# Score products with full-height rests in an fp32 diffusion-transformer kernel

## The chip, the cores and the metric

The kernel runs on one core of one Trainium2 chip. The metric is device time in microseconds (us): the median of several executions. One further execution was recorded by the hardware profiler; its span runs from its first to its last instruction.

## What is computed

Two layers of a hybrid backbone over 256 latent and 256 context tokens of width 1024, all fp32. Each layer modulates its input (adaLN), projects it once, and splits the result into three head groups of 64-wide heads: A (6 query heads on 2 key heads, a window of 128 tokens and a per-head sink), B (4 heads, a neighbourhood with a relative bias), C (6 query heads on 2 key heads, global, normalised queries and keys). Latent queries also see all context keys; context queries see context keys alone. An output projection, a norm, and a mixture of 16 experts follow. The part that the change touches is the first line of each attention:

```python
s = jnp.einsum('bqhgd,bkhd->bhgqk', q_i, k_all, preferred_element_type=jnp.float32) * scale
p = jax.nn.softmax(s, -1).astype(v.dtype)
return jnp.einsum('bhgqk,bkhd->bqhgd', p, v_all).reshape(bsz, Q_BLOCK, n_heads * HEAD_DIM)
```

In the second (last) layer no context queries are needed.

## The kernel before, in words

Large products run in the type fp32r. To keep fp32's digits, an operand is split into a head (its value rounded to fp32r) and a rest (what rounding left over), and products of the parts are added in one PSUM bank. The three products of `mm3` (L221 to L223) are head by head, head by rest and rest by head. The weights are split by `split_w`: ScalarE casts 1024 columns to the head `wh` (L211), VectorE subtracts it to give the rest `wl` (L212). Both lie in the pool `wsp`, which holds three such pairs, and each pair serves two of the eight contraction steps of a projection, for four token tiles of 128.

Projection comes in the order V, A, C, B. For each token tile, `finish` rotates and normalises queries and keys, splits them into `hl`, transposes `hl` in blocks of 128 columns on PE (L725, up to four blocks in one bank `qtp`) and evicts them into `qkA`, `qkB` or `qkC`. A query head takes one block, in which the 64 rows of its head and the 64 rows of its rest stand one above the other, the head on top for even heads and below for odd ones. A key head takes one block with its head twice, so a single product over 128 rows gives (query head + query rest) by key head. The key rests stand once, two key heads to a block. The second score product takes only the 64 rows with the query's head and the key's rest (L523); `kv % 2` says which half.

For one head and one block of 128 queries, `products` writes one bank `s`. For latent queries (`nb == 1`) it holds 512 keys: L516 is the first product, for group A L520 adds the window's mask as a bf16 product, and L523 is the second. Context queries (`nb == 2`, layer 0 alone: banks A2, A3, C2, C3, B2) have two query blocks of 256 keys each in one bank. `scores` takes the maximum on VectorE (L535) and the exponential on ScalarE (L546). `values` transposes the probabilities in four pieces (L559, bank `ptp`), copies them (L490 on ScalarE, one in six L492 on VectorE) and multiplies by the values in 16 products with 64 columns each (L568). `blocks` keeps two or three heads pending between the two. The adaLN products (L366, 32 columns) are put between. With `PAIRS="B"`, group B of layer 1 issues the products of two heads before their scores.

The output projection reads its weights in eight pieces `w_half`: the first three are split into `wsp` as attention ends, the others into buffers of their own (L911), each ordered behind the last attention transposes (`otp`, L865, cast at L868). For the experts, buffers that are free by then become 15 slots of 1 MB for weights: three of them are the pairs of `wsp`, one is `ringc`.

The order on each engine is not written by hand: the framework orders the program by a simulated timeline, under the dependencies and priorities given, and any change of the code orders it anew.

Of the kernel before, what the change touches and what calls it, by code (L numbers as in the profile page):

```python
# [17 lines left out]
F32 = mybir.dt.float32  # L18
F32R = mybir.dt.float32r
# [4 lines left out]
ALU = mybir.AluOpType  # L24
# [4 lines left out]
P = 128  # L29
# [18 lines left out]
RING_B = 4  # L48
WS_UNITS = 3
VECS_AHEAD = 2  # L50
# [8 lines left out]
P_BUFS = 3  # L59
KN = [dict(ADA=("10101010", "00100100", "01010101", "01", "110"), AHEAD=(2, 3, 2), EVAC="VSSSSS", PAIRS=""), dict(ADA=("01010101", "01010101", "11110000", "10", "0"), AHEAD=(2, 3, 2), EVAC="VSSSSS", PAIRS="B")]  # L60
REST_G = ((1, 2, 3), (0, 1))
# [48 lines left out]
def layers(ctx: ExitStack, tc: tile.TileContext, x_in, x_ctx, c_in, w_in, w_out, w_ada, rows_in, lnv, sink, gains, rpbp,  # L110
# [12 lines left out]
    ringu = ctx.enter_context(tc.tile_pool(name="ringu", bufs=RING_U))  # L123
    wsp = ctx.enter_context(tc.tile_pool(name="wsp", bufs=3))
    sm = ctx.enter_context(tc.tile_pool(name="sm", bufs=6))
# [329 lines left out]
    def pre_moe(l, sb, sr):  # L455
# [5 lines left out]
        with ExitStack() as st, ExitStack() as su:  # L461
            with ExitStack() as sa:
# [39 lines left out]

                def products(ps, bk, hs):

                    grp, b, nb = bk.grp, bk.b, bk.nb
                    qk, nq = qkt[grp], heads[grp]
                    tiles = [ps.tile([P, 512], F32, tag="s", name="s") for _ in hs]
                    k = slice(0, 512) if nb == 1 else slice(256, 512)  # L510
                    for c in range(nb):
                        q = slice((b + c) * P, (b + c + 1) * P)
                        each = [(h, h if grp == "B" else h % 2, s if nb == 1 else s[:, c * 256:(c + 1) * 256])
                                for h, s in zip(hs, tiles)]
                        for h, kv, so in each:
                            T.matmul(so, qk[:, h, q], qk[:, nq + kv, k], start=True, stop=False)  # L516
                        if nb == 1 and grp == "A":
                            o = 128 * (1 - b)
                            for s in tiles:
                                T.matmul(s[:, o:o + 128], identb, maskb[:, b], start=False, stop=False)  # L520
                        for h, kv, so in each:
                            r = slice(64 * (kv % 2), 64 * (kv % 2) + 64)
                            T.matmul(so, qk[r, h, q], qk[r, 8 + kv // 2, k], start=False, stop=True)  # L523
                    return tiles

# [65 lines left out]
                def blocks(keys, depth):  # L591

                    for key in keys:
                        if key in banks:
                            bk = Bank(key)
                            n = 2 if bk.grp in KN[l]["PAIRS"] else 1
                            for h0 in range(bk.h0, bk.h1, n):
                                hs = range(h0, h0 + n)
                                for h, s in zip(hs, products(now["ps"], bk, hs)):
                                    pend.append((bk, h, scores(bk, h, s)))  # L600
                                    drain(now["ps"], now["po"], depth)
                                    yield

# [6 lines left out]
                with ExitStack() as sp:  # L610
# [68 lines left out]
                    def finish(grp, t, src, lo, rs=None):  # L679
# [5 lines left out]
                        if grp not in qkt:  # L685
                            qkt[grp] = ap_.tile([P, 10, N_TOK], F32R, tag="qkC" if grp == "C" else "qkAB",
                                                name=f"qk{grp}")
                        if grp == "A" and t < 2:
                            src = rope(src, t, 0, 8, cosx[:, t], sinx[:, t])
                        elif grp == "C":  # L690
                            for h0, h1, i in ((0, 6, 0), (6, 8, 2)):
# [7 lines left out]
                                else:  # L699
# [5 lines left out]
                                    [P, n, HD]), op=ALU.mult)  # L705
                        hl = wq.tile([P, 1280], F32R, tag="hl", name="hl")
                        if lo == 0:
# [8 lines left out]
                        S.copy(hh, sv.unsqueeze(2).to_broadcast([P, nk, 2, HD]))  # L716
                        V.tensor_tensor(out=hl[:, kd:kd + nk * HD].rearrange("p (h d) -> p h d", d=HD), in0=sv,
                                        in1=hh[:, :, 0].bitcast(F32), op=ALU.subtract)
                        a = 0 if lo == 0 else nq
                        n = 8 + nk // 2  # L720
                        while a < n:
# [174 lines left out]
            def w_half(kt):  # L896
                if kt % 2 == 0:
                    whl.append(unit(w_out[l, kt // 2]))
                w = whl[kt // 2][:, kt % 2 * 1024:kt % 2 * 1024 + 1024]
                if kt < 3:  # L900

                    hl = split_w(w)
                    for split, last_of in zip((keep["cast"], keep["split"]), heads_done[kt - 3]):
                        order(split, last_of, mybir.DependencyClass.NoSync)
                    return hl
# [350 lines left out]
    def moe(l, ringb, gen, rt, u2d, aff, nt, sb, ahead):  # L1256
        cap = CAP[l]
        with ExitStack() as st:
            mp = st.enter_context(tc.tile_pool(name="moe", bufs=1, side="right"))
            ringc = st.enter_context(tc.tile_pool(name="ringc", bufs=1))  # L1260
            m1 = st.enter_context(tc.tile_pool(name="moe1", bufs=2))
# [15 lines left out]
            for e in range(NE - 2):  # L1277
# [4 lines left out]
            slots = [(ring, "w")] * RING_A + [(ringu, "wu")] * (RING_U - 1) + [(ringb[0], "wb")] + [  # L1282
                (ringb[1], "wb")] * (RING_B - 1) + [None] * WS_UNITS + [(ringc, "wb"), (ringu, "wu")]
            n_slots = len(slots)
# [347 lines left out]
```

## Time and profile before

| | us |
|---|---|
| median of 3 runs | 1159.81 |
| lowest and highest | 1156.51, 1160.08 |
| the profiled execution | 1151.46 |
| its span | 1149.6 |
| PE busy | 1032.0 (90%) |
| VectorE (DVE) busy | 518.2 (45%) |
| ScalarE (ACT) busy | 330.1 (29%) |
| GpSimd (POOL) busy | 257.0 (22%) |

The mean granted clock of TensorE is 0.962. Each row of a timeline is an instruction (or several alike): its start, its length, engine, line, operation, output and inputs by the program's names, the shape of the weights x the moving operand, and in brackets the idle time before it and what ended it. `64*128 64x512` is a product with weights of 64 rows and 128 columns and 512 moving columns. PEld is the load of weights, which can run under a product. In the waits, `A <- B: 1.6, 1, 1.6` says that A waited for B 1.6 us in total, in one wait, the longest of 1.6 us.

### The profile page before, as it was taken

To read this page: it belongs to the slowest core of one execution; us is meant where nothing else is said; L and a number is where in the kernel's file an instruction comes from. 1 tells how busy PE (TensorE), PEld (TensorE's weight loads), DVE (VectorE), ACT (ScalarE), POOL (GpSimd) and SP (SyncE) were. 2 spreads that over 40 slices of the span, in tenths; PEclk is the share of its full clock that TensorE was granted. 3 is DMA by queue.
4 is the path that set the end of the run, shared out by engine and by line. 5 is a ranking of instruction groups with operands and counts; after the bars stand their busy time and mean duration, and the time that the engine had idled before them with its cause. 6 is when DMAs were issued, how large, how long until landed. Compare 5 with 4: busy or idle time off the path is not lost. (4 is left out here: it accounts for less than half of the span.)

```text
span 1149.6 us, 21044 instructions
## 1 busy us (share of the span) xinstructions
PE 1032.0 (90%) x8651; PEld 598.5 (52%) x8652; DVE 518.2 (45%) x1221; ACT 330.1 (29%) x688; POOL 257.0 (22%) x238
## 2 busy tenths in 40 slices
PE   5899999999968999999997799999995999878775
PEld 3677666667854444444443478666673333322222
DVE  2525655557782443443433644655865122211115
ACT  1334457456121110110111543446632001000002
POOL 3000000100004244244233300001001455434142
PEclk9999999999988999999999799999996999989997
DMA  9855442864698999999996345574398999999992
GB/s 315 314 191 157 141 146 76 295 229 182 233 418 272 371 369 361 375 347 337 344 370 247 131 147 193 188 257 144 118 381 336 328 395 394 397 393 392 407 390 85
DMA packets 67345, 320.93 MB, mean 279 GB/s; under 512 B 14894, under 2 KB 19086, under 8 KB 38312
## 3 DMA queue, kind: packets, MB, share of 16 engines
q1 hardware_dynamic: 50304, 289.21, 66.2%
q0 software_dynamic: 11136, 23.30, 7.7%
q10 hardware_dynamic: 5800, 6.97, 1.8%
q8 instruction: 71, 1.16, 0.4%
q14 instruction: 34, 0.28, 0.1%
HBM read 310.40 MB, written 18.15 MB: 286 GB/s over the span
## 5 line engine op out<-in xcount | busy, mean ns | idle before, releaser
L1184 PE MATMUL ha<-w,xT 128*32 128x512 f32 (+1 forms) x1512 | 251.1, 604 | 22.1 <-DMA w<-in_w_dram 21.7
L1184 PEld LDWEIGHTS ha<-w,xT 128*32 128x32 f32 (+1 forms) x1512 | 74.4, 121 | 165.3 <-issue 117.0
L1211 ACT ACTIVATE hs<-ha 64x512 f32<-64x512 f32 x32 | 18.9, 592 | 403.4 <-PE ha L1184 403.4
L1184 PE MATMUL ya<-w,gT 128*32 128x512 f32 (+1 forms) x768 | 128.3, 597 | 2.7 <-DVE y L1231 1.6
L221 PE MATMUL pj<-wh,u 128*128 128x512 f32 (+2 forms) x256 | 95.1, 384 | 5.1 <-ACT wh L211 3.8
L222 PE MATMUL pj<-wl,u 128*128 128x512 f32 (+2 forms) x256 | 96.2, 377 | 0.6 <-DVE wl L212 0.5
L223 PE MATMUL pj<-wh,u 128*128 128x512 f32 (+2 forms) x256 | 93.2, 376 | 0.0
L1156 POOL MEMSET xg<- 96x1024 f32 (+1 forms) x32 | 30.2, 947 | 216.2 <-PE tp L1169 133.5
L1253 POOL DMA_INDIRECT ysum<-y,ii x30 | 44.2, 1474 | 148.1 <-DVE y L1234 98.9
L1231 DVE TENSOR_TENSOR y<-ya,gt 64x512 f32<-64x512 f32 x60 | 41.3, 688 | 78.8 <-PE ya L1184 71.2
L535 DVE TENSOR_REDUCE mx<-s 128x1 f32<-128x512 f32 (+1 forms) x80 | 54.7, 690 | 42.4 <-PE s L523 41.6
L212 DVE TENSOR_TENSOR wl<-w,wh 128x1024 fp32r<-128x1024 f32 x38 | 46.0, 1223 | 51.5 <-ACT wh L211 51.5
L1212 DVE TENSOR_TENSOR hs<-hs,ha 64x512 f32<-64x512 f32 x32 | 22.1, 690 | 102.9 <-ACT hs L1211 102.7
L546 ACT ACTIVATE p<-s,nm 128x512 f32<-128x512 f32 (+1 forms) x96 | 59.3, 624 | 30.5 <-DVE nm L542 18.1
L1184 PEld LDWEIGHTS ya<-w,gT 128*32 128x32 f32 (+1 forms) x768 | 34.5, 118 | 54.6 <-issue 45.1
L1190 PE MATMUL hb<-w,xT 128*32 128x256 f32 x1008 | 62.7, 379 | 0.0
L221 PEld LDWEIGHTS pj<-wh,u 128*128 128x128 f32 x256 | 48.4, 191 | 20.1 <-ACT wh L211 4.7
L211 ACT CAST wh<-w 128x1024 fp32r<-128x1024 f32 x38 | 39.2, 1051 | 66.1 <-DMA w<-in_w_in_dram 42.7
L568 PE MATMUL o<-vt,pt 128*64 128x64 f32 x1280 | 51.6, 227 | 3.3 <-ACT pt L490 3.3
L222 PEld LDWEIGHTS pj<-wl,u 128*128 128x128 f32 x256 | 49.0, 191 | 10.0 <-DVE wl L212 1.7
L223 PEld LDWEIGHTS pj<-wh,u 128*128 128x128 f32 x256 | 48.7, 191 | 10.0 <-issue 1.1
L1239 POOL TENSOR_SCALAR gt<-xs,gs 96x1024 f32<-96x1024 f32 x16 | 53.3, 3332 | 0.0
(295 smaller groups left out, 1684.7 us busy)
## 6 DMA issues: line engine op xcount, KB each, us to landing
w<-in_w_dram SPq DMA_DIRECT2D x152, 1024.0 KB
w<-in_w_ada_dram SPq DMA_DIRECT2D x44, 1024.0 KB
w<-in_w_dram SPq DMA_DIRECT2D x76, 512.0 KB
w<-in_w_in_dram SPq DMA_DIRECT2D x16, 1024.0 KB
w<-in_w_out_dram SPq DMA_DIRECT2D x8, 1024.0 KB
early<-in_w_ada_dram SPq DMA_DIRECT2D x4, 1024.0 KB
y<-modd POOLq DMA_DIRECT2D x6, 512.0 KB, 4.4
u2d<-u SPq DMA_DIRECT2D x6, 512.0 KB
```

Of the source, the lines that this page charges most:

```text
L212: keep["split"] = d = eng.tensor_tensor(out=lo, in0=w, in1=h.bitcast(F32), op=ALU.subtract)
L221: T.matmul(out_, ah, bh, start=start, stop=False)
L222: T.matmul(out_, ah, bl, start=False, stop=False)
L223: keep["product"] = T.matmul(out_, al, bh, start=False, stop=stop)
L535: greatest = V.reduce_max(out=mx[:, :nb], in_=s.rearrange("p (b k) -> p b k", b=nb), axis=AX.X)
L546: power = S.activation(out=p_[:, c * w:(c + 1) * w], in_=s[:, c * w:(c + 1) * w], func=AF.Exp, scale=scale, bias=bk.nm[:, c, i:i + 1], acc ...
L568: T.matmul(bk.o[q:q + 64, oc:oc + HD], pt[:, (c * nk + k) * P + q:(c * nk + k) * P + q + 64], vt[:, (2 * (nb - 1)) + k, v0:v0 + HD], start ...
L1184: keep["product"] = T.matmul(a[64 * m + t0:64 * m + t1], x[:, kt, t0:t1], w(m, kt), start=(kt == 0), stop=(kt == n - 1))
L1190: keep["product"] = T.matmul(b[c:c + self.cap - 64, 0:256], x[:, kt, 64:], w(m, kt)[:, hf * 256:hf * 256 + 256], start=(kt == 0), stop=(kt ...
L1231: V.tensor_tensor(out=out_[:n, half[m]], in0=a[64 * m:64 * m + n], in1=g[:n, half[m]], op=ALU.mult)
L1239: order(G.tensor_scalar(out=g[:self.cap], in0=self.bcs[0][:self.cap], scalar1=gs[:self.cap, 0:1], scalar2=None, op0=ALU.mult), keep["gathe ...
L1253: G.indirect_dma_start(dst, bass.IndirectOffsetOnAxis(ap=ii[:cap], axis=0), y[:cap], None, bounds_check=self.nt * P - 1, oob_is_err=False, ...
```

## The change

The key rests are kept twice, one above the other, in a block of their own for each key head, as the key heads are. The second score product then uses all 128 rows and also adds query rest by key rest. Group A's mask moves behind it. `hl` and the tile of group B grow, so there are 8 + `nk` blocks to transpose and not 8 + `nk // 2` (`nk` is 2 for A and C, 4 for B). `PAIRS` is gone. The pool `wsp` holds two pairs; the third piece of w_out is split with the later ones (L905 in the changed file), and `ringc` has two slots.

```diff
-WS_UNITS = 3
+WS_UNITS = 2
...
-    wsp = ctx.enter_context(tc.tile_pool(name="wsp", bufs=3))
+    wsp = ctx.enter_context(tc.tile_pool(name="wsp", bufs=WS_UNITS))
...
-                def products(ps, bk, hs):
+                def products(ps, bk, h):
...
-                        for h, kv, so in each:
-                            T.matmul(so, qk[:, h, q], qk[:, nq + kv, k], start=True, stop=False)
-                        if nb == 1 and grp == "A":
-                            o = 128 * (1 - b)
-                            for s in tiles:
-                                T.matmul(s[:, o:o + 128], identb, maskb[:, b], start=False, stop=False)
-                        for h, kv, so in each:
-                            r = slice(64 * (kv % 2), 64 * (kv % 2) + 64)
-                            T.matmul(so, qk[r, h, q], qk[r, 8 + kv // 2, k], start=False, stop=True)
-                    return tiles
+                        so = s if nb == 1 else s[:, c * 256:(c + 1) * 256]
+                        T.matmul(so, qk[:, h, q], qk[:, nq + kv, k], start=True, stop=False)
+                        T.matmul(so, qk[:, h, q], qk[:, 8 + kv, k], start=False, stop=nb == 2 or grp != "A")
+                    if nb == 1 and grp == "A":
+                        o = 128 * (1 - b)
+                        T.matmul(s[:, o:o + 128], identb, maskb[:, b], start=False, stop=True)
+                    return s
...
-                            n = 2 if bk.grp in KN[l]["PAIRS"] else 1
-                            for h0 in range(bk.h0, bk.h1, n):
-                                hs = range(h0, h0 + n)
-                                for h, s in zip(hs, products(now["ps"], bk, hs)):
-                                    pend.append((bk, h, scores(bk, h, s)))
-                                    drain(now["ps"], now["po"], depth)
-                                    yield
+                            for h in range(bk.h0, bk.h1):
+                                pend.append((bk, h, scores(bk, h, products(now["ps"], bk, h))))
+                                drain(now["ps"], now["po"], depth)
+                                yield
...
-                            qkt[grp] = ap_.tile([P, 10, N_TOK], F32R, tag="qkC" if grp == "C" else "qkAB",
+                            qkt[grp] = ap_.tile([P, 8 + nk, N_TOK], F32R, tag="qkC" if grp == "C" else "qkAB",
...
-                        hl = wq.tile([P, 1280], F32R, tag="hl", name="hl")
+                        hl = wq.tile([P, 1536], F32R, tag="hl", name="hl")
...
-                        V.tensor_tensor(out=hl[:, kd:kd + nk * HD].rearrange("p (h d) -> p h d", d=HD), in0=sv,
-                                        in1=hh[:, :, 0].bitcast(F32), op=ALU.subtract)
+                        V.tensor_tensor(out=hl[:, kd:kd + nk * 2 * HD].rearrange("p (h x d) -> p h x d", x=2, d=HD),
+                                        in0=sv.unsqueeze(2).to_broadcast([P, nk, 2, HD]), in1=hh.bitcast(F32),
+                                        op=ALU.subtract)
...
-                        n = 8 + nk // 2
+                        n = 8 + nk
...
-                if kt < 3:
-
+                if kt < WS_UNITS:
                     hl = split_w(w)
+
...
-            ringc = st.enter_context(tc.tile_pool(name="ringc", bufs=1))
+            ringc = st.enter_context(tc.tile_pool(name="ringc", bufs=2))
...
-                (ringb[1], "wb")] * (RING_B - 1) + [None] * WS_UNITS + [(ringc, "wb"), (ringu, "wu")]
+                (ringb[1], "wb")] * (RING_B - 1) + [None] * WS_UNITS + [(ringc, "wb")] * 2 + [(ringu, "wu")]
```

The change makes the order anew. On PE, in group B of layer 1, the heads stood like this before (`s` is the bank of one head, `qkB` its queries and keys; L568 are value products, L559 transposes of probabilities):

```order
L516 MATMUL s_8496<-qkB_8069 128x512
L523 MATMUL s_8496<-qkB_8069 128x512
L516 MATMUL s_8495<-qkB_8069 128x512
L523 MATMUL s_8495<-qkB_8069 128x512
L568 MATMUL o_8430<-vt_6801,pt_8460 64x64 x8
L559 MATMUL ptp_8507<-cst_75,p_8428 128x128 x4
```

and stand like this now (L515 and L516 are the two score products, L555 the transposes, L564 the value products):

```order
L515 MATMUL s_8514<-qkB_8080 128x512
L516 MATMUL s_8514<-qkB_8080 128x512
L555 MATMUL ptp_8523<-cst_75,p_8447 128x128 x4
L564 MATMUL o_8449<-vt_6804,pt_8479 64x64 x8
L515 MATMUL s_8553<-qkB_8080 128x512
L516 MATMUL s_8553<-qkB_8080 128x512
```

In both the two products of one head follow each other; the two heads at the start of the group no longer do.

On ACT, where layer 1's attention ends and its output projection begins, this stood before (`wh` are pieces of w_out in `wsp`, `hl` those in other buffers, `o` the attention output, `pt` probabilities):

```order
L211 CAST wh<-w 128x1024 x2
L490 COPY pt<-ptp 128x512
L546 ACTIVATE p,z<-s,nm 128x512
L211 CAST wh<-w 128x1024
L490 COPY pt<-ptp 128x512
L868 CAST o<-otp 128x512 x2
L490 COPY pt<-ptp 128x512
L868 CAST o<-otp 128x512 x2
L911 CAST hl<-w 128x1024 x5
```

and this stands there now:

```order
L211 CAST wh<-w 128x1024
L542 ACTIVATE p,z<-s,nm 128x512
L211 CAST wh<-w 128x1024
L542 ACTIVATE p,z<-s,nm 128x512
L490 COPY pt<-ptp 128x512
L862 CAST o<-otp 128x512
L490 COPY pt<-ptp 128x512
L862 CAST o<-otp 128x512 x3
L905 CAST hl<-w 128x1024 x6
```

One of the three early casts has moved behind the last cast of the attention output.

More of the change, by code (lines that the diff above doesn't have):

```diff
@@ L59 @@
 P_BUFS = 3
-KN = [dict(ADA=("10101010", "00100100", "01010101", "01", "110"), AHEAD=(2, 3, 2), EVAC="VSSSSS", PAIRS=""), dict(ADA=("01010101", "01010101", "11110000", "10", "0"), AHEAD=(2, 3, 2), EVAC="VSSSSS", PAIRS="B")]
+KN = [dict(ADA=("10101010", "00100100", "01010101", "01", "110"), AHEAD=(2, 3, 2), EVAC="VSSSSS"), dict(ADA=("01010101", "01010101", "11110000", "10", "0"), AHEAD=(2, 3, 2), EVAC="VSSSSS")]
 REST_G = ((1, 2, 3), (0, 1))
@@ L501, in __init__ @@
                         self.z = sm.tile([P, self.nb, self.nh], F32, tag="z", name="z", bufs=3)
-                def products(ps, bk, hs):
+                def products(ps, bk, h):
                     grp, b, nb = bk.grp, bk.b, bk.nb
                     qk, nq = qkt[grp], heads[grp]
-                    tiles = [ps.tile([P, 512], F32, tag="s", name="s") for _ in hs]
+                    kv = h if grp == "B" else h % 2
+                    s = ps.tile([P, 512], F32, tag="s", name="s")
                     k = slice(0, 512) if nb == 1 else slice(256, 512)
@@ L512, in products @@
                         q = slice((b + c) * P, (b + c + 1) * P)
-                        each = [(h, h if grp == "B" else h % 2, s if nb == 1 else s[:, c * 256:(c + 1) * 256])
-                                for h, s in zip(hs, tiles)]
-                        for h, kv, so in each:
-                            T.matmul(so, qk[:, h, q], qk[:, nq + kv, k], start=True, stop=False)
-                        if nb == 1 and grp == "A":
-                            o = 128 * (1 - b)
-                            for s in tiles:
-                                T.matmul(s[:, o:o + 128], identb, maskb[:, b], start=False, stop=False)
-                        for h, kv, so in each:
-                            r = slice(64 * (kv % 2), 64 * (kv % 2) + 64)
-                            T.matmul(so, qk[r, h, q], qk[r, 8 + kv // 2, k], start=False, stop=True)
-                    return tiles
+                        so = s if nb == 1 else s[:, c * 256:(c + 1) * 256]
[5 more added lines that the diff above has]
+                    return s
                 def scores(bk, h, s):
```

## The prediction

> **What bounds the kernel now.** I read the table by stretches first, for the two layers' attention. Columns: start and end, length, then busy us (and instructions) of PE, PEld, DVE, ACT and POOL, the granted clock, the DMA share and GB/s.
>
> ```profile
> 118.00:183.00 65.00, 61.47 (x536) 42.45 (x535) 35.65 (x92) 34.94 (x89) 0.68 (x1) 1.00 0.35 117
> 183.00:262.00 79.00, 79.00 (x898) 50.89 (x897) 45.49 (x125) 42.56 (x114) 6.33 (x11) 1.00 0.62 216
> ...
> 783.00:830.00 47.00, 46.32 (x542) 31.35 (x538) 32.34 (x88) 28.78 (x69) 5.50 (x10) 1.00 0.45 158
> ```
>
> PE is busy almost throughout, at full clock; DVE and ACT are busy for about 60% of it, and DMA is below its limit. A busy PE need not be the bound, so the second view is who waits. PE's own waits, first for layer 0 (115 to 262 us; first and last of four rows, 3.4 us together), then for layer 1 (690 to 840 us; first and last of seven, 5.8 us together):
>
> ```profile
> PE pj L221 <- ACT wh L211: 1.6, 1, 1.6
> ...
> PE ptp L559 <- ACT p L546: 0.4, 1, 0.4
> ```
> ```profile
> PE o L568 <- ACT pt L490: 1.9, 3, 1.1
> ...
> PE qtp L725 <- ACT qkC L490: 0.3, 1, 0.3
> ```
>
> In the other direction, between 80 and 262 us, the waits are far longer:
>
> ```profile
> ACT pt L490 <- PE ptp L559: 29.5, 18, 5.0
> ...
> DVE mx L535 <- PE s L523: 28.9, 28, 3.7
> ```
>
> So attention is bound by PE's instruction stream, and what shortens that stream shortens the stage. Third view: the timeline of PE, read by starts and not by durations, since the ends of matmuls are modelled. Four products of group B in layer 1:
>
> ```profile
> 812.04 0.48 PE L516 MATMUL s<-qkB 128*128 128x512 f32 x1
> 812.45 0.50 PE L523 MATMUL s<-qkB 64*128 64x512 f32 x1
> 812.88 0.51 PE L516 MATMUL s<-qkB 128*128 128x512 f32 x1
> 813.32 0.49 PE L523 MATMUL s<-qkB 64*128 64x512 f32 x1
> 813.74 0.69 PE L568 MATMUL o<-vt,pt 128*64 128x64 f32 x16
> ```
>
> The durations are alike, and each start is 0.41 to 0.44 us after the last. Now the same 512 columns of the same type where both neighbours use 128 rows and 128 columns, from the output projection of layer 0:
>
> ```profile
> 276.02 0.40 PE L221 MATMUL oacc<-wh,o 128*128 128x512 f32 x1
> 276.25 0.39 PE L222 MATMUL oacc<-wl,o 128*128 128x512 f32 x1
> ```
>
> Here it is 0.23. Going into a 64-row product costs some 0.18 us and coming out some 0.20, and the weight load shows why: it starts with its matmul, not under the one before.
>
> ```profile
> 820.63 0.18 PEld L523 LDWEIGHTS s<-qkB 64*128 64x128 f32 x1 [0.24 <-issue]
> ```
>
> **The change: the score products.** How many there are, by the source line:
>
> ```profile
> L523 PE MATMUL s<-qkA x36: 378/492/503, 123.0 to 780.9; 64*128 64x512 f32 x24, 64*128 64x256 f32 x12
> ...
> L523 PE MATMUL s<-qkC x36: 378/491/503, 184.1 to 811.2; 64*128 64x512 f32 x24, 64*128 64x256 f32 x12
> ...
> L523 PE MATMUL s<-qkB x24: 377/492/502, 218.5 to 827.1; 64*128 64x512 f32 x16, 64*128 64x256 f32 x8
> ```
>
> Groups B and C with 512 columns: 24 + 16 = 40. From first product to rest 0.41 becomes 0.23: 40 x 0.18 = 7.2 us. From rest to what follows, 0.43 becomes 0.23 only if the follower uses all 128 columns; where it is a value product or an adaLN product, which use 64 or 32, a step remains:
>
> ```profile
> 145.68 0.40 PE L223 MATMUL pj<-wh,u 128*128 128x512 f32 x1
> 146.01 0.51 PE L568 MATMUL o<-vt,pt 128*64 128x64 f32 x10
> ```
>
> That is 0.33. In PE's order before, 19 of the 64 rests with 512 columns are followed so, 45 are not: (45 x 0.20 + 19 x 0.10) / 64 = 0.17 each, and 40 x 0.17 = 6.8 us.
>
> Group A has its mask between the two products:
>
> ```profile
> 759.75 0.45 PE L725 MATMUL qtp<-identr,hl 128*128 128x128 f32 x3
> 760.03 0.47 PE L516 MATMUL s<-qkA 128*128 128x512 f32 x1
> 760.34 0.23 PE L520 MATMUL s<-cbf 128*128 128x128 bf16 x1
> 760.50 0.49 PE L523 MATMUL s<-qkA 64*128 64x512 f32 x1
> 760.92 0.66 PE L559 MATMUL ptp<-cst,p 128*128 128x128 f32 x4
> ```
>
> From the first start to the transposes 0.89 us. After: 0.23 to the rest, 0.31 to the mask, and I keep the 0.16 behind the mask: 0.70, so 24 x 0.19 = 4.6 us.
>
> With 256 columns there are 12 + 12 + 8 = 32, all in layer 0. Beside them two neighbours of 128 rows:
>
> ```profile
> 259.01 0.36 PE L516 MATMUL s<-qkB 128*128 128x256 f32 x1
> 259.31 0.38 PE L523 MATMUL s<-qkB 64*128 64x256 f32 x1
> 259.61 0.38 PE L516 MATMUL s<-qkB 128*128 128x256 f32 x1
> ```
> ```profile
> 773.09 0.28 PE L221 MATMUL pj<-wh,u 128*128 128x256 f32 x1
> 773.20 0.28 PE L222 MATMUL pj<-wl,u 128*128 128x256 f32 x1
> ```
>
> 0.30 against 0.11 to 0.12: 0.19 less into the rest, 32 x 0.19 = 6.1 us; out of it 0.19 for 25 and 0.10 for the 7 that a narrow product follows, 5.5 us. Together 7.2 + 6.8 + 4.6 + 11.6 = 30.2 us of PE, 20.9 in layer 0 and 9.3 in layer 1.
>
> By the Trainium skill ("TensorE: Matmul & The Clock Gate", the table "Why this matters for your kernels") products on few rows that lie in distinct row groups run concurrently, which speaks against the change: rests of an even and an odd key head could share one slot. By that rule the four pairs of rests of group B in layer 1 would hide 4 x 0.4 = 1.6 us and the gain would be 28.6 instead of 30.2. The rows at 812 us show what the old kernel gets of it: the order puts a full product or another step between any two rests, so there is nothing to lose.
>
> **Transposes.** Each group has 4 token tiles per layer; A and C get one transpose more per tile, B two: 16 per layer, 32 in all. Three take 0.28 us in the rows at 759.75 (start to next start), so 32 x 0.093 = 3.0 us back. The number of evictions stays; some get wider, as do the VectorE subtractions, both on engines with 40% to spare: nothing.
>
> **One pair of split tiles less.** A pair costs a cast and a subtraction:
>
> ```profile
> L212 DVE TENSOR_TENSOR wl<-w,wh 128x1024 fp32r<-128x1024 f32 x38 | 46.0, 1223 | 51.5 <-ACT wh L211 51.5
> ...
> L211 ACT CAST wh<-w 128x1024 fp32r<-128x1024 f32 x38 | 39.2, 1051 | 66.1 <-DMA w<-in_w_in_dram 42.7 <-PE pj L223 23.4
> ```
>
> 1.05 + 1.22 = 2.3 us, and PE uses a pair for 24 products of 0.23 = 5.5 us. With two pairs the next is split while the other is used, 3.2 us ahead. That is the cover. Behind a cast that waits for PE stand the copies and exponentials of ACT's queue, and PE waits for those; but the row says that casts mostly wait for weights. In attention, where ACT has other work between, I take 2 us of new waits, from -1 (one cast of 1.05 less ahead of layer 1's modulation in ACT's queue) to +8 (8 of the 32 pairs of both layers late by one cast).
>
> **The output projection.** The third half of w_out is split only after the last attention transposes are cast, with six casts in a row instead of five. In layer 1 PE has already run dry there:
>
> ```profile
> 839.72 0.71 PE L865 MATMUL otp<-cst,xs 128*128 128x128 f32 x5
> 842.09 0.50 PE L221 MATMUL oacc<-hl,o 128*128 128x512 f32 x1 [1.67 <-ACT hl L911]
> ```
>
> There the six products that leave the front come back behind it, and the wait stays. In layer 0 fewer products cover the same casts: +1 us, from 0 to 2.5. The weight slots of the experts are as many as before, and their loads start behind this point, so the DMA stream of the experts moves earlier with it.
>
> **What does not arrive.** Once PE is faster, the softmax chain may be late. Prices per head:
>
> ```profile
> L546 ACT ACTIVATE p<-s,nm 128x512 f32<-128x512 f32 x64 | 44.2, 692 | 24.7 <-DVE nm L542 13.9 <-PE ptp L559 5.3 <-DVE nm L539 3.4
> ...
> L490 ACT COPY pt<-ptp 128x512 f32<-128x512 f32 x68 | 39.8, 593 | 45.1 <-PE ptp L559 44.4
> ...
> L546 ACT ACTIVATION_READ_ACCUMULATOR p<-s,nm 128x1 f32 x96 | 19.7, 205 | 0.0
> ...
> L546 ACT ACTIVATE p<-s,nm 128x256 f32<-128x256 f32 x32 | 15.1, 488 | 5.8 <-DVE nm L542 4.1 <-DVE z L578 1.4 <-DVE nm L539 0.2
> ```
>
> ACT: 0.69 + 0.20 + 5/6 of 0.59 = 1.39 us for a head of 512 columns, 2 x (0.49 + 0.20) + 0.49 = 1.87 for two blocks of 256. PE after the change: 0.46 for two wide products (0.48 for four narrow ones), four transposes at 0.093, and at most the 0.69 of the row at 813.74 for the values: 1.5 us, and adaLN products between. So the narrow heads may become ACT's, and the others stay PE's with little to spare. The saving in the two stretches that hold little but attention is that of 40 wide heads of B and C at 0.35 and of the 10 narrow ones of C2, C3 and B2 at 0.73 (two blocks each, 11.6 / 32 for one): 14.2 us between 183 and 262 and 7.0 between 783 and 830. I take a quarter of that, 5 us, as lost; the bounds are 0 and 14, as if layer 0's stretch gained nothing.
>
> Sum: -30.2 + 3.0 + 2 + 1 + 5 = -19.2 us. The profiled execution took 1151.46 us (span 1149.6), so it would take 1132.3; the median of the runs, 1159.81, is 0.7% above it, and I take the same difference from it: 1140.6.
>
> **Rivals.** First, the chain: the heads of both stretches run at the pace of ACT and of the steps between, and 14 instead of 5 us are lost: -10, 1150. For it speaks the count per head; against it, that ACT and DVE now have 40% idle, nearly all of it waiting for PE. The Trainium skill ("TensorEngine Tiling (Array Packing)", section "PSUM Bottleneck") says that after a faster TensorE the copies out of PSUM may be next; no row here shows that yet.
>
> Second, slower: the split. If a cast stands behind late work in ACT's queue until its pair is needed, PE waits the whole 2.3 us. There are 32 pairs in the projections; it decides from 21.2 / 2.3 = 9 of them on, and with half of them exposed 16 x 2.3 = 37 us are lost against 21 gained: 1175. Against it: PE's longest such wait is 1.6 us.
>
> Third, the change does not do what it says: the 0.41 comes from writing one bank twice, not from the rows. Then only the 3.0 + 2 + 1 remain: 1166. Against it: the projection adds to one bank at 0.23.
>
> Fourth, no difference: the scheduler orders the whole program anew, and a worse order in the projections eats the gain.
>
> **Chances.** Forecast 0.64, chain 0.22, neither way 0.06, the split 0.05, no saving 0.03. About 0.3%, 3.5 us, is what a measurement of this kernel can tell from no change. Faster by more: 0.86; within: 0.06; slower: 0.08. The range goes from everything arriving (27.2 us of PE and the 1 us at the start of layer 1: 1131) to the chain with 2.5 us more in the waits (1152).
>
> **What would show it.** In the changed kernel, starts of the two products 0.23 apart (0.12 with 256 columns), loads of the second under the first; PE's waits in attention up from 9 to about 15 us, mostly on exponentials and copies; the output projection of layer 0 starting 15 us earlier, that of layer 1 about 20. If the starts stay at 0.41, the third rival holds; if PE's rows wait for wh and wl by 10 us or more, the second.

## The result, and the profile after

| us | before | after |
|---|---|---|
| first comparison: median (lowest to highest, runs) | 1158.74 (1156.51 to 1160.08, 4) | 1140.69 (1139.29 to 1141.36, 4) |
| ratio, 95% interval | | 0.9838 [0.9804, 0.9871] |
| second comparison, with the last experiments | 1157.00 (1152.56 to 1167.72, 14) | 1145.31 (1141.55 to 1147.34, 6) |
| ratio, 95% interval | | 0.9883 [0.9847, 0.9919] |
| span of the profiled execution | 1149.6 | 1137.5 |
| PE busy | 1032.0 | 1017.5 |

The change makes the kernel 1.2 to 1.6% faster. The forecast was 1140.6. The second comparison is part of the reading: medians of one and the same kernel differ by 4.6 us, so where two experiments lie less than some 5 us apart, nothing is made of it.

The profiled execution of before was also short for its kind: an unchanged copy (the run `same`, below) spanned 1159.0. The granted clock accounts for that: before spent 88.1 us at a clock of 0.50 and `same` 109.6, and half of the difference, an estimate that is worked out below, is 10.7 us. Where stretches are compared, `same` stands for before.

First view, the same three stretches of attention as before (the changed kernel reaches the later ones sooner, so the windows are moved and shortened; columns as in the prediction):

```profile
118.00:183.00 65.00, 61.65 (x582) 46.97 (x581) 45.69 (x116) 40.77 (x99) 0.68 (x1) 1.00 0.41 132
183.00:250.00 67.00, 67.00 (x882) 47.16 (x881) 43.70 (x118) 39.82 (x104) 6.31 (x11) 1.00 0.72 255
772.00:818.00 46.00, 43.62 (x600) 33.40 (x600) 35.34 (x89) 29.67 (x70) 5.49 (x10) 1.00 0.44 162
```

In layer 0 PE is still busy to the brim and still the bound, now in a window of 67 us where it was 79. In layer 1 it is idle for 2.4 of 46 us: there a second limit shows.

Second view, PE's timeline for a head of group B in layer 1, from its first product to the next head's:

```profile
803.40 0.48 PE L515 MATMUL s<-qkB 128*128 128x512 f32 x1
803.72 0.40 PE L516 MATMUL s<-qkB 128*128 128x512 f32 x1
803.96 0.60 PE L555 MATMUL ptp<-cst,p 128*128 128x128 f32 x4
804.49 0.69 PE L564 MATMUL o<-vt,pt 128*64 128x64 f32 x16
805.10 0.50 PE L515 MATMUL s<-qkB 128*128 128x512 f32 x1
```

The second product's successor starts 0.24 us behind it, where it was 0.41 to 0.44. The first product's successor, however, starts 0.32 behind, not 0.23. The weight loads (PEld) now run under the product before, as was asked of them: the second one's load starts at 803.49, while the first product, started at 803.40, is running.

```profile
803.38 0.19 PEld L515 LDWEIGHTS s<-qkB 128*128 128x128 f32 x1
803.49 0.19 PEld L516 LDWEIGHTS s<-qkB 128*128 128x128 f32 x1
```

The Trainium skill ("TensorE: Matmul & The Clock Gate", "The mechanism") says in its list of what overlaps that a weight load overlaps a running matmul only when the row groups differ. The same section of the Trainium skill also lets a load for the background weight buffer be pulled ahead. These two rows do not fit the list: both use all 128 rows, and the load is early; the 64-row load of the kernel before, quoted in the prediction, was late. The measurement decides.

Third view, PE's waits in layer 1 (680 to 820 us; the first three of eight rows, which add up to 10.3 us; layer 0, 115 to 250 us, has 3.2):

```profile
PE pj L221 <- ACT wh L211: 3.2, 3, 1.5
PE ptp L555 <- ACT p L542: 2.7, 3, 1.9
PE s L515 <- ACT p L542: 1.3, 1, 1.3
```

They wait for casts and exponentials, and in the rows left out for copies: 13.5 us in both layers together.

### The profile page after: what moved, and what is told of

The parts are those of the page before. It is cut to its first block, busy times and chain, and to the rows that moved or that the text cites. A ratio compares the mean times of both kernels' runs of the same rounds, so it can differ in the third digit from the quotient of the medians.

```text
span 1137.5 us, 21098 instructions
## 1 busy us (share of the span) xinstructions
PE 1017.5 (89%) x8683; PEld 597.6 (53%) x8684; DVE 522.4 (46%) x1221; ACT 332.6 (29%) x688; POOL 257.0 (23%) x238
## 5 line engine op out<-in xcount | busy, mean ns | idle before, releaser
L1178 PE MATMUL ha<-w,xT 128*32 128x512 f32 (+1 forms) x1512 | 252.5, 613 | 17.7 <-DMA w<-in_w_dram 17.2
L1178 PE MATMUL ya<-w,gT 128*32 128x512 f32 (+1 forms) x768 | 124.8, 597 | 3.2 <-DVE y L1225 1.6
L221 PE MATMUL pj<-wh,u 128*128 128x512 f32 (+2 forms) x256 | 93.1, 389 | 4.8 <-ACT wh L211 3.2
L223 PE MATMUL pj<-wh,u 128*128 128x512 f32 (+2 forms) x256 | 92.6, 376 | 0.0
L212 DVE TENSOR_TENSOR wl<-w,wh 128x1024 fp32r<-128x1024 f32 x36 | 43.7, 1221 | 50.3 <-ACT wh L211 50.2
L222 PEld LDWEIGHTS pj<-wl,u 128*128 128x128 f32 x256 | 49.7, 194 | 10.2 <-issue 1.6
L564 PE MATMUL o<-vt,pt 128*64 128x64 f32 x1280 | 52.7, 227 | 1.8 <-ACT pt L490 1.1
L555 PE MATMUL ptp<-cst,p 128*128 128x128 f32 x320 | 50.6, 279 | 3.4 <-ACT p L542 3.1
```

The source lines that it names most:

```text
L212: keep["split"] = d = eng.tensor_tensor(out=lo, in0=w, in1=h.bitcast(F32), op=ALU.subtract)
L221: T.matmul(out_, ah, bh, start=start, stop=False)
L222: T.matmul(out_, ah, bl, start=False, stop=False)
L223: keep["product"] = T.matmul(out_, al, bh, start=False, stop=stop)
L555: T.transpose(tp[:, k * P:(k + 1) * P], p_[:, k * P:(k + 1) * P], ident)
L564: T.matmul(bk.o[q:q + 64, oc:oc + HD], pt[:, (c * nk + k) * P + q:(c * nk + k) * P + q + 64], vt[:, (2 * (nb - 1)) + k, v0:v0 + HD], start ...
```

## The experiments

A stretch, below, runs from the first projection product of a layer to its last product of the output projection, or from there to the next layer's first; the starts are those of PE's timeline. In brackets stands the part of it in us at a granted clock of 0.50. The last column has the median of all runs. Rows64, pool2, nopairs and same were measured beside a before of 1159.94 us, the three named toep and after_vfull beside 1159.44, and after_again, after_one, after_half and pool2_one, on another chip, beside 1157.00; the ratios are to these.

| us | layer 0 | experts and norm | layer 1 | to the end | median |
|---|---|---|---|---|---|
| same (before) | 305.4 (3.4) | 340.4 | 203.0 (9.8) | 288.5 | 1160.92 |
| nopairs | 309.0 (10.2) | 337.0 | 204.0 (6.3) | 289.1 | 1159.68 |
| after | 293.3 (6.8) | 336.8 | 198.4 (6.8) | 288.1 | 1140.69 |
| after_again | 296.9 (10.2) | 336.5 | 198.9 (6.7) | 286.6 | 1145.31 |
| rows64 | 314.1 (10.2) | 336.5 | 204.9 (10.1) | 288.4 | 1168.88 |
| pool2 | 311.6 (10.2) | 343.9 | 204.1 (9.4) | 286.8 | 1170.57 |
| pool2_toep | 307.4 (6.8) | 345.0 | 203.6 (9.4) | 289.0 | 1166.47 |
| pool2_one | 304.7 (0) | 344.9 | 200.8 (5.0) | 287.2 | 1167.86 |
| before_toep | 298.9 (0) | 339.9 | 203.3 (13.6) | 288.4 | 1152.44 |
| after_toep | 293.2 (3.4) | 340.0 | 207.1 (23.0) | 287.9 | 1146.36 |
| after_one | 290.0 (0) | 340.1 | 197.5 (6.0) | 287.3 | 1143.65 |
| after_half | 292.5 (3.4) | 340.7 | 204.3 (16.7) | 287.7 | 1146.43 |
| after_vfull | 304.6 (6.8) | 338.3 | 204.2 (9.8) | 284.4 | 1160.80 |

After_again is the changed kernel once more, and its layer 0 is 3.6 us longer; so single differences under 4 us mean little. The clock is a large part of this scatter. The profiled execution of before has 303.7 us for layer 0, `same` 305.4 and nopairs, which is changed in layer 1 alone, 309.0. They spent 0, 3.4 and 10.2 us of it at 0.50. Projection products start 0.43 apart there (after_half at 713 us) and 0.23 at full clock, so I estimate the loss at half of that time; without it the three are 303.7, 303.7 and 303.9.

Theory: the rows of the second product are what counts, the rest of the change costs a little, and some of the gain is lost to the softmax chain. Rivals: the saving comes from somewhere else than the rows, or the cost of the lost pair is of another size.

**rows64.** The changed kernel, with the second product back on 64 rows; all else, PE's order too, is that of after.

```diff
-T.matmul(so, qk[:, h, q], qk[:, 8 + kv, k], start=False, stop=nb == 2 or grp != "A")
+r = slice(64 * (kv % 2), 64 * (kv % 2) + 64)
+T.matmul(so, qk[r, h, q], qk[r, 8 + kv, k], start=False, stop=nb == 2 or grp != "A")
```

> The changed kernel with one line set back: the second score product reads the 64 rows of before from the doubled tiles; transposes, pools and the order on PE are those of the changed kernel. If the height of that product is what pays, the starts of the products go back to 0.41 us apart and the score products take about 27 us more of PE, of which some 7 us fall into waits that PE now has: 1158 to 1162 us. If the gain came from the new order, the pools or the missing pairs, it stays near 1141.

Measured: 1168.88 (1164.45 to 1174.02, 12 runs), ratio to before 1.0079 [1.0053, 1.0106]. That is above the 1158 to 1162 that were expected. So the rows alone bring 28.2 us against the first median of after and 23.6 against the second, and everything else in the change costs 8.9 (6 to 12 by the interval). With PE's order the same in both, whole cycles can be laid side by side. The head of group B:

```profile
832.90 0.50 PE L515 MATMUL s<-qkB 128*128 128x512 f32 x1
833.33 0.50 PE L517 MATMUL s<-qkB 64*128 64x512 f32 x1
833.76 0.66 PE L556 MATMUL ptp<-cst,p 128*128 128x128 f32 x4
834.34 0.69 PE L565 MATMUL o<-vt,pt 128*64 128x64 f32 x16
834.96 0.50 PE L515 MATMUL s<-qkB 128*128 128x512 f32 x1
```

2.06 us from head to head, 1.70 in after: 0.36 a head. Group A with its mask, first in rows64, then in after, at the same place of the order:

```profile
794.66 0.47 PE L515 MATMUL s<-qkA 128*128 128x512 f32 x1
795.06 0.49 PE L517 MATMUL s<-qkA 64*128 64x512 f32 x1
795.49 0.23 PE L520 MATMUL s<-cbf 128*128 128x128 bf16 x1
795.52 0.47 PE L515 MATMUL s<-qkC 128*128 128x512 f32 x1
```
```profile
770.40 0.48 PE L515 MATMUL s<-qkA 128*128 128x512 f32 x1
770.71 0.40 PE L516 MATMUL s<-qkA 128*128 128x512 f32 x1
770.95 0.23 PE L519 MATMUL s<-cbf 128*128 128x128 bf16 x1
770.99 0.47 PE L515 MATMUL s<-qkC 128*128 128x512 f32 x1
```

0.86 against 0.59: 0.27 a head. Two narrow blocks of group B in layer 0, in `same` and in after, up to the value products behind them:

```profile
263.23 0.36 PE L516 MATMUL s<-qkB 128*128 128x256 f32 x1
...
264.46 1.62 PE L568 MATMUL o<-vt,pt 128*64 128x64 f32 x48
```
```profile
248.05 0.36 PE L515 MATMUL s<-qkB 128*128 128x256 f32 x1
...
248.70 0.51 PE L564 MATMUL o<-vt,pt 128*64 128x64 f32 x10
```

1.23 against 0.65: 0.58 for two. So the sum is 40 x 0.36 + 24 x 0.27 + 16 x 0.58 = 14.4 + 6.5 + 9.3 = 30.2 us. One head of each kind is scaled up here; the median over all heads, rows64 against after, is 0.32 for B and 0.35 for C with 512 columns and 0.28 for A. The rival that the saving has nothing to do with the rows falls. By the stretches of the table layer 0 gets 20.8 us of it and layer 1 6.5; against after_again it is 17.2 and 6.0.

**pool2.** The kernel before, with the pool part of the change alone: two pairs of split weights, the third piece of w_out split late, two slots in `ringc`.

```diff
-WS_UNITS = 3
+WS_UNITS = 2
...
-                if kt < 3:
+                if kt < WS_UNITS:
...
-            ringc = st.enter_context(tc.tile_pool(name="ringc", bufs=1))
+            ringc = st.enter_context(tc.tile_pool(name="ringc", bufs=2))
...
```

> The kernel before with the pool part alone: two pairs of split tiles, the third piece of w_out split later, two slots in ringc. My sum puts 3 us on it (2 for waits on wh and wl, 1 in the output projection): 1161 to 1163. The rival of the late split wants 10 us or more, with PE waiting for wh or wl over 10 us. No price: 1159.

Measured: 1170.57 (6 runs), ratio 1.0082 [1.0049, 1.0114]: 9.5 us slower by the ratio, not 3. By the table some 6 us of it lie in layer 0, about half of them by the clock, and 3.5 between the layers. The place in layer 0 is the same in after: at 87 us ACT issues eight transfers that spread the neighbourhood bias (`spread_bias`, L280) in a row. ACT's timeline in after (the line ends with the wait that this makes for the next cast):

```profile
87.06 7.94 ACTq L280 DMA_DIRECT2D toep<-in_rpb_dram  x8
95.04 0.51 ACT L704 CAST hl<-t 128x384 fp32r<-128x384 f32 x1 [7.40 <-DMA toep<-in_rpb_dram]
```

No weight is split meanwhile, so PE lives on the pairs that are ready. In `same` the eight issues hold ACT even longer, 10.55 us from 85.41 on, and PE starts its last projection product ahead of the wait at 95.86; with two pairs, in after, that is at 92.07. Then PE waits for `hl`, the split queries and keys, whose casts stand behind the issues as well. First `same`, then after:

```profile
PE qtp L725 <- DVE hl L712: 1.0, 1, 1.0
```
```profile
PE qtp L719 <- DVE hl L705: 3.8, 1, 3.8
```

In the windows the wait has a sequel in the granted clock (the column after POOL's). First `same`, then after:

```profile
95.00:100.00 5.00, 3.58 (x20) 2.40 (x19) 2.96 (x6) 4.00 (x9) 0.00 (x0) 1.00 0.35 78
100.00:105.00 5.00, 5.00 (x28) 4.19 (x28) 2.15 (x4) 0.79 (x3) 0.00 (x0) 1.00 0.54 208
```
```profile
90.00:95.00 5.00, 2.45 (x11) 1.69 (x9) 0.00 (x0) 0.00 (x0) 0.00 (x0) 0.96 0.54 119
95.00:100.00 5.00, 3.71 (x19) 3.25 (x19) 4.15 (x7) 4.90 (x10) 0.00 (x0) 0.50 0.27 60
100.00:105.00 5.00, 5.00 (x23) 4.21 (x23) 1.32 (x3) 1.09 (x2) 0.00 (x0) 0.85 0.60 210
```

PE does 19 and 23 instructions in the last two windows at clocks of 0.50 and 0.85. The Trainium skill ("TensorE: Matmul & The Clock Gate", "Why this matters for your kernels") asks for no idle gap of TensorE over about 3 us, or it falls to half clock; the trace agrees, with 3.8 us followed by 0.50 and 1.0 us followed by 1.00. A long wait is not the only way into the half clock, though. In nopairs it lasts 6.8 us from 155.9 us on, and from 140 us to there no wait of PE is longer than 0.4 us:

```profile
155.00:160.00 5.00, 5.00 (x17) 2.75 (x20) 1.58 (x5) 0.47 (x2) 0.00 (x0) 0.59 0.01 3
```

What sets it off there was not found.

The 3.5 us between the layers go with the order that pool2 got, not with the number of pairs: its first transposes of layer 1 wait for the norm's small steps on DVE, where after and rows64, which have two pairs as well, wait 4.1 us for the last copy, as `same` does. Pool2:

```profile
PE xtp L646 <- DVE a L260: 7.5, 1, 7.5
```

**nopairs and same.** The kernel before without `PAIRS="B"`, and the kernel before unchanged.

```diff
-AHEAD=(2, 3, 2), EVAC="VSSSSS", PAIRS="B")]
+AHEAD=(2, 3, 2), EVAC="VSSSSS", PAIRS="")]
```

> The kernel before with PAIRS empty in layer 1 as well, nothing else. The prediction has it at nothing: within 1 us of the kernel before. If rests of two heads did run side by side in pairs, 1.6 us slower.

> The kernel before, unchanged, as a second profile and a second set of times. The profiled execution on which the prediction rests took 1151.5 us, below all timed ones. If that was one lucky execution, this profile has a span near 1157 and shows where the 5 to 7 us lie; the ratio should be 1.000.

Measured: nopairs 1159.68 (12 runs), ratio 0.9996 [0.9973, 1.0019]; same 1160.92, ratio 1.0000 [0.9973, 1.0027]. Issuing heads in pairs shows no worth, and taking it away no cost; the 1.6 us of the other case lie inside the interval, so the times alone do not exclude them. The order does: nowhere on PE in before do two rests stand next to each other. Where the microseconds lie by which the profiled execution of before was short, `same` shows as well: in the clock, as said above.

**before_toep, pool2_toep, after_toep.** Three kernels (before, pool2, after) with the eight transfers issued on GpSimd's queue.

```diff
-        tc.keep_in_program_order(S.dma_start(toep[lh].rearrange("q r k -> r q k"),
+        tc.keep_in_program_order(G.dma_start(toep[lh].rearrange("q r k -> r q k"),
```

> The kernel before with the same eight issues moved to GpSimd's queue. With three pairs PE waited there 0 to 1.0 us: 1157 to 1159, at most 2 us faster than before. If moving these DMAs is worth as much here as in the changed kernel, the third pair was no cover for them.

> The kernel before with the pool part alone and these issues moved. The pool part alone cost 9.5 us; about 6 of it should go (4.0 of PE's wait and the half clock behind it), the 4 us at the start of layer 1 stay: 1164. If the price is waits on wh and wl everywhere, nothing changes: 1170.

> The changed kernel with its eight bias-spreading DMAs issued from GpSimd's queue instead of ScalarE's. In the changed kernel these issues hold ACT for 7.4 us at 87 us, PE then waits 3.8 us for the casts behind them and runs at half clock for some 5 us. If that is the price of the missing pair in layer 0, both go: 1134 to 1136 us. If the price lies elsewhere, 1141.

Measured: before_toep 1152.44 (12 runs), ratio 0.9937 [0.9915, 0.9958]; pool2_toep 1166.47 (12 runs), ratio 1.0058 [1.0035, 1.0081]; after_toep 1146.36 (6 runs), ratio 0.9876 [0.9838, 0.9914]. Two of the expectations missed, and pool2_toep lies between its two. Before gains 7 us though its third pair was held to be cover enough. PE's listed waits in its layer 0 (from the first projection product on) fall from 8.3 to 5.0 us, half of the 6.5 us by which the stretch shortens; the half clock that `same` has there and before_toep has not is worth some 1.7; where the rest comes from was not found. Pool2 gains about 4 us, which its intervals do not tell from nothing. So moving the issues is worth no more with two pairs than with three, and it does not take away the price of the lost pair: pool2_toep is 14.0 us slower than before_toep, and pool2 was 10.6 slower than before.

After gains nothing, although its 3.8 us wait and the half clock are gone. The waits of after_toep tell where it went in the profiled execution, which is the slowest of the six (1151.20 us). First DVE (198 to 207 us, then 798 to 810), then PE (798 to 810):

```profile
DVE b L341 <- DMA modd<-g: 3.1, 1, 3.1
```
```profile
DVE xs L874 <- DMA lnb<-in_lnv_dram: 4.7, 1, 4.7
```
```profile
PE o L564 <- DVE pt L492: 3.7, 1, 3.7
```

Two transfers, of 4 KB and of 512 KB, land late. DVE is held behind them and PE behind DVE. The first of these waits is not due to the move: after_again, where nothing was moved, has it too (PE waits 2.3 us there, as here). The second has no equal in after, after_again, after_one and after_half (1.1 us of DVE at most), and layer 1 becomes 8.7 us longer, most of it by the clock (23.0 us at 0.50 against 6.8). The DMA share is 1.03 at the second wait, but after has 0.98 and 1.01 at that place and waits 0.7 us, so that full transfer queues make the landing late is not shown.

**after_one, pool2_one, after_half, after_again.** The eight issues left on ACT's queue, but one in each of the first eight steps of group C's projection (after_one, pool2_one), or four in each layer (after_half), and after itself once more.

```diff
-                    if l == 0:
-                        for lh in range(L * 4):
-                            spread_bias(lh)
...
                         modulation(1, i)
+                        if l == 0 and i < L * 4:
+                            spread_bias(i)
```

> The changed kernel, with the eight bias-spread transfers still issued on ACT's queue, but one in each of the first eight steps of the projection of group C instead of all eight in a row after the projection of group A. Theory 'the row of issues': eight issues of 0.92 us in a row hold ACT for 7.4 us at 87 to 95 us, two split pairs do not last that long, TensorE waits 3.8 us and its granted clock is 0.50 and 0.85 in the ten microseconds after. One issue at a time lets the splits through: the 3.8 us wait is under 1 us, the clock is 1.00 from 85 to 115 us, and the time is 1133 to 1137 us. Rival 'the transfers' (what the transfers meet later decides, as with the issues on GpSimd's queue): wait and clock improve just the same, but the gain is lost by 215 us or in layer 1, and the time is 1140 to 1147 us.

> The kernel before with two pairs of split tiles and two tiles of the other ring (the run pool2), and the same spreading out of the eight issues. Theory 'the row of issues': the loss of the third pair is dear only because of the row of issues, so pool2's 1170.6 us falls by 5 to 8 us, to 1162 to 1165. Rival 'the pairs': two pairs are late in other places too (layer 1's start, 4 us there), and the time stays at 1167 to 1171 us.

> The changed kernel, with the four issues for layer 0's bias where all eight stood, and the four for layer 1's at the same place of layer 1. Theory 'the row of issues': half the row holds ACT for 3.7 us, which two pairs cover; the wait in layer 0 falls from 3.8 to under 1 us and the time by 3 to 5 us, if the row in layer 1 is covered as well: 1136 to 1138 us. Rival 'a new row': layer 1's projections pay what layer 0's saved, 1140 to 1143 us.

> The changed kernel itself, once more, beside the others of this set. 1139 to 1142 us if the four times it has are typical of it (median 1140.69); 1143 or more if they were lucky, as the profiled execution of the kernel before was (span 1149.6 where an unchanged copy showed 1159.0). The part-by-part sums then move by the same amount.

Measured, side by side: after_again 1145.31 (6 runs), after_one 1143.65 (1139.06 to 1147.04, 6 runs), after_half 1146.43 (1140.43 to 1149.10, 6 runs), pool2_one 1167.86 (1160.32 to 1169.60, 9 runs); ratios 0.9883, 0.9871 [0.9835, 0.9907], 0.9883 [0.9845, 0.9920] and 1.0074 [1.0044, 1.0104]. None differs from its partner by what can be told. After_one and pool2_one miss the times of the theory and fall on those of their rivals, after_half misses both. Yet the wait is gone in after_one, and the clock stays at 1.00:

```profile
90.00:95.00 5.00, 5.00 (x24) 4.14 (x23) 3.42 (x7) 2.33 (x5) 0.00 (x0) 1.00 0.71 223
95.00:100.00 5.00, 5.00 (x30) 4.19 (x29) 2.44 (x4) 1.84 (x5) 0.00 (x0) 1.00 0.30 86
```

By the table its layer 0 is 3.3 us shorter than after's, and pool2_one's 6.9 us shorter than pool2's, which is back at the length of `same`. All of the 3.3 us and some 5 of the 6.9 can be the clock. So the row of issues makes the 3.8 us wait and the half clock behind it. That it is the price of the lost pair is not shown: a kernel with three pairs and the issues spread out was not run, with the issues moved it gains 6.5 us in layer 0, and the medians of the two-pair kernels do not fall by what can be told. After_one is 1.8 us ahead of after at the end of layer 0's output projection and 3.8 at the last weights of layer 0's experts. PE's timeline there, first after_one, then after:

```profile
594.73 0.55 PE L1163 MATMUL tp<-cst,hs 96*128 96x96 f32 x4
596.18 1.05 PE L1178 MATMUL ha<-w,xT 128*32 128x512 f32 x4 [0.90 <-DMA w<-in_w_dram]
598.66 3.20 PE L1178 MATMUL ha<-w,xT 128*32 128x512 f32 x26 [1.42 <-DMA w<-in_w_dram]
```
```profile
598.51 0.55 PE L1163 MATMUL tp<-cst,hs 96*128 96x96 f32 x4
598.99 3.64 PE L1178 MATMUL ha<-w,xT 128*32 128x512 f32 x32
```

After_one has its transposes (`tp`) done 3.8 us sooner, comes too early for its weights, waits twice, and is some 0.8 us ahead when it goes on; the DMA share in its windows there is 0.95 and 1.01. After_toep waits at the same place for 2.3 us. After gets to the same products at 598.99 and waits for nothing. So in these executions after arrives about when the weights do, and a still faster layer 0 meets a stream of transfers that is full. That is the rival 'the transfers', though not at the places that it names. In after_half the same lead is not seen; its layer 1 is 204.3 us long against 198.4. The trace shows the rival 'a new row' there. The four issues hold ACT for 7.5 us, not 3.7, PE waits for the weights cast behind them, and a clock of 0.50 for 6.8 us follows. PE:

```profile
711.11 1.54 PE L221 MATMUL pj<-wh,u 128*128 128x512 f32 x4 [3.45 <-ACT wh L211]
```

**after_vfull.** The changed kernel, with the value products on all 128 query columns: 8 per head instead of 16.

```diff
-for q in range(0, P, 64):
-    T.matmul(bk.o[q:q + 64, oc:oc + HD],
-             pt[:, (c * nk + k) * P + q:(c * nk + k) * P + q + 64],
-             vt[:, (2 * (nb - 1)) + k, v0:v0 + HD], start=(k == 0), stop=(k == nk - 1))
+T.matmul(bk.o[:, oc:oc + HD], pt[:, (c * nk + k) * P:(c * nk + k + 1) * P],
+         vt[:, (2 * (nb - 1)) + k, v0:v0 + HD], start=(k == 0), stop=(k == nk - 1))
```

> The changed kernel with the value products on all 128 columns: 4 products per head instead of 16 on 64 columns in two column groups. If a change of the shape of the weights costs 0.1 us as it does between rows, and a full product of 64 moving columns starts 0.11 us after the last one, a head takes 0.44 instead of 0.60 us and 0.1 less around it: some 20 us of PE for 80 heads, of which half or more should arrive: 1121 to 1131. If the softmax chain now bounds attention, 1137 or more.

Measured: 1160.80 (12 runs), ratio to before 1.0006 [0.9982, 1.0030]: 15 to 20 us slower than after. The view of groups, first after_vfull, then after:

```profile
L563 PE MATMUL o<-vt,pt 128*128 128x64 f32 x640 | 82.3, 274 | 1.8 <-ACT pt L490 1.4 <-DVE pt L492 0.2
```
```profile
L564 PE MATMUL o<-vt,pt 128*64 128x64 f32 x1280 | 52.7, 227 | 1.8 <-ACT pt L490 1.1 <-DVE pt L492 0.2
```

Half as many products keep PE busy 30 us longer. The expectation had counted 4 products per head, the kernel's calls, where the trace has 8; at its own 0.11 us each they take 0.88 and not 0.44, more than the 0.60 of the 16 narrow ones. So using the whole array does not pay by itself: it paid for products with 512 and 256 moving columns, and not for these with 64.

## Why the prediction was right

**The score products, -30.2.** Measured by whole cycles: 30.2. That the two agree to the decimal is luck. The terms inside are off by up to 2.3 us and cancel: B and C with 512 columns 14.4 (forecast 7.2 + 6.8), group A 6.5 (4.6), the narrow blocks 9.3 (11.6). Group A was too low because the gap behind the mask was kept at its old 0.16; it is 0.04 in after's rows above. The narrow ones were too high because the first product of the two blocks still takes 0.20 (248.05 to 248.25) and not 0.12, and the step to the value product behind them 0.21.

**The starts.** "0.23 apart" held from the second product on and not from the first: its successor comes after 0.32 wherever fp32 transposes or narrow products stand ahead, and so part of the 0.41 of before never belonged to the 64-row product. What was asked too much there came back at the other end: in the head of group B the transposes' successor moved from 0.58 to 0.53, and the second product's from 0.43 to 0.24. The cycle was right, its division was not.

**What does not arrive, 5.** Against rows64, whose listed waits in layer 1 are 6.6 us, after's 10.3 are 3.7 more; in layer 0 it is 3.2 against 2.8. Together 4.1, so the size held. The place held in part: two thirds of it were put into layer 0, where 17 to 21 of the 20.9 us of PE arrived (20.8 in this pair of executions, of which some 1.7 are the clock; 17.2 against after_again). In layer 1 about 6 of 9.3 arrived, and there it lies in the waits for casts, exponentials and copies. PE's waits were to rise to about 15 us; they are 13.5.

**Transposes, +3.0.** PE's busy time on them went from 23.4 (192 of them, `same`) to 27.0 (224), 3.6 for 32, by durations that overlap. No run has the transposes alone, so their 3.0 is not shown by itself.

**One pair less, +2, and the output projection, +1.** This is the term that was mis-sized: together 3 were forecast and 9.5 measured when done alone. The prediction took a late cast for the danger and the cover of 3.2 us for enough. At 87 us what uses up the cover is no cast: it is eight transfer issues in a row on ACT, 7.9 us, and the half clock behind the 3.8 us wait. The trace of before holds that row too, for 9.68 us; it was not priced, because PE waited only 0.4 us there. That is a part of the price, not all of it: pool2 also waits longer between the layers, and taking the row away did not bring the times of the two-pair kernels back. Where the rest lies stays open. The upper end of the term, +8 and +2.5, holds the 9.5. The output projection itself was right: the waits for its casts went from 0 to 0.6 us in layer 0 and from 1.7 to 1.9 in layer 1.

**The sum.** In after the whole of what is not rows costs 8.9 us (rows64 against before) instead of 6, and rows less waits bring 23.6 to 28.2 instead of 25.2. Both are within what the runs can tell. In the first comparison the two errors of 3 us cancel, which is luck; in the second the kernel gains 11.7 us by the medians and not 19.2, and the time is still inside the range. The starts of the output projection, 15 and 20 us earlier by the forecast, moved by 14.9 and 19.6 between `same` and after (9.9 and 14.4 in after_again). First `same`, then after, in each layer:

```profile
276.50 0.48 PE L221 MATMUL oacc<-wh,o 128*128 128x512 f32 x1
...
843.27 0.50 PE L221 MATMUL oacc<-wh,o 128*128 128x512 f32 x1
```
```profile
261.56 0.48 PE L221 MATMUL oacc<-wh,o 128*128 128x512 f32 x1
...
823.68 0.50 PE L221 MATMUL oacc<-wh,o 128*128 128x512 f32 x1
```

Against the profiled execution of before they would be 13 and 12 us, because that one was short by 9.4 us of span. Taking the difference of the sum from the median, and not the profiled time itself, is what kept the forecast right: 1151.46 less 19.2 would have been 1132.3.

**The rivals.** The chain as bound: only a part of it, in layer 1. The late split: waits for `wh` are 3.2 us in layer 1, not 10, though the 3.8 us wait for `hl` is of its kind. No saving by rows: ruled out by rows64. A worse order that eats the gain: not in after, though pool2 shows that an order can cost 3.5 us at a place far from the edit.

## What to carry to other kernels

Price a change of tile shape by a whole cycle of the order (head to head, same neighbours), since what a shape costs is spread over the starts before and behind it. Before giving up a buffer that runs ahead, look for the longest stretch in which its producer does something else, issues of transfers included, and compare the cover with that and not with the mean. Run an unchanged copy before building on one execution, and compare the time at the lower clock before explaining a few us. When a compute-bound stretch has been shortened, see whether the transfer stream behind it still keeps up: from there on savings are given back.

## What the runs showed of the hardware beyond that

- Eight issues in a row of a transfer from DRAM to DRAM on ACT's queue took 7.94 us in after, 9.68 in before and 10.55 in `same`, and but for a copy that was under way at their start in after, ACT did nothing else. Most of the issues that stand alone in after_one take 0.76 us.
- Value products whose weights have 64 columns follow one another every 0.038 us (16 from 804.49 to 805.10), those with 128 columns every 0.10 (8 from 811.87 to 812.68 in after_vfull):

```profile
811.87 1.00 PE L563 MATMUL o<-vt,pt 128*128 128x64 f32 x8
812.68 0.48 PE L515 MATMUL s<-qkC 128*128 128x512 f32 x1
```

  The weight loads go with that: eight loads of 128 columns took 0.97 us there, and sixteen of 64 columns 0.55 in after. That they set the pace is likely but not shown.
- A wait of PE of 3.8 us was followed by granted clocks of 0.50 and 0.85 over ten microseconds; one of 1.0 us left it at 1.00. Drops to 0.50 for 3.4 or 6.8 us also came without a long wait, and not in every execution of the same kernel: at 155 us `same` has one and before has none.
